# A decoder layer on one core: an inverse in two pieces, its gathers halved in number, tables made early, another order of loads

## The chip, the cores and the metric

The kernel is one launch on one core of a Trainium2 chip. The core's engines are TensorE (PE in the profile; PEld is its loading of weights), VectorE (DVE), ScalarE (ACT), GpSimd (POOL) and SyncE (SP), which issues the DMAs. The metric is the device time of the launch in microseconds (us), lower is better.

## The reference, cut to what matters

The kernel computes one decoder layer over 1,024 tokens of width 1,024 (depth 1, batch 1). A normed input is projected by one matrix of 3,136 columns. 448 of them feed multi-head latent attention with four heads, 1,664 feed an RWKV-7 recurrence of eight heads of 64 and the two low-rank inputs of its decay and rate, and 1,024 are a gate.

```python
u = rmsnorm(h, norm_pre_g[l])
p_mla, p_rw, z = jnp.split(u @ w_in[l], [MLA_COLS, MLA_COLS + RW_SHIFT_COLS], axis=-1)
c_q, c_kv, k_r = jnp.split(p_mla, [Q_LORA, Q_LORA + KV_LORA], axis=-1)
q  = rmsnorm(c_q, mla_q_norm_g[l]) @ mla_w_uq[l]      # split in nope and rope parts, per head
kv = rmsnorm(c_kv, mla_kv_norm_g[l]) @ mla_w_ukv[l]
y_mla = mla_attention(q_nope, apply_rope(q_rope, cos, sin), k_nope, apply_rope(k_r, cos, sin), v_mla)

ps = p_rw + (token_shift(p_rw) - p_rw) * rw_mu[l]
r, k, v, xw, xa = jnp.split(ps, ...)
w_log = -jax.nn.softplus(-(rw_w0[l] + jnp.tanh(xw) @ rw_w2[l])) - 0.5
decay, a = jnp.exp(-jnp.exp(w_log)), jax.nn.sigmoid(rw_a0[l] + xa @ rw_a2[l])
# kk: k * rw_k_k, normalised per head; k: k * (1 + (a - 1) * rw_k_a)
# per token and head: S = S * w + (S @ -kk) (kk * a)^T + v k^T ;  y = S @ r
y = wkv7_scan(r_h, heads(decay), k_h, v_h, kk, heads(a))
# y: group norm per head, plus (r * k * rw_r_k summed over the head) * v

y_cat = jnp.concatenate([y_mla, y_rw], axis=-1) * jax.nn.silu(z)
h = h + rmsnorm(y_cat @ w_out[l], norm_post_g[l])
```

## The kernel before, in words

The sequence is worked in two halves of 512 tokens. The recurrence isn't run token by token: it is cut into eight chunks of 64 tokens for each half, and within a chunk a 64x64 triangular system has to be inverted for each head. The recurrence, and with it the inverse, is done first for one half, then for the other; attention and the output come behind both.

**Order of the work.** `PROGRAM` (lines 132 to 136) is a string of operations in which they are written down; a scheduler (`schedule_with_timeline_sim`, line 42) then interleaves the instructions of all of them on every engine, by a simulation of its own. Once chosen, each engine's order is fixed, and an instruction that waits holds up whatever stands behind it on its engine. `BEHIND` (line 139) adds constraints: the operation named first is issued only after the last instruction that the other one returned. The letters, with the half as the first digit:

- `A` (`stage_a`, 165): loads four blocks of 128 tokens of x, norms them (eight scalings of 128x512 on VectorE, line 181), turns them with 32 transposes on TensorE (188), and writes the result as `uH` (ScalarE, 192, the rounded value) and `uL` (VectorE, 193, what the rounding lost), 16 pieces of each. Every projection multiplies in three terms: `uH` and `uL` by the weight's high part, `uH` by its low part.
- `X` (`lora_in`, 246): one projection (`proj`, 214: 24 matmuls of 512 columns, line 221, behind a load `wf`, a cast on ScalarE, 201, and eight subtractions on GpSimd, 211), its token shift (`v`, 228 to 231), a tanh (250) and the split `xw`, `xa` for the low-rank products (262, 263).
- `P` with the column block 0 to 3 (`prep`, 281): low-rank products, then the projections of k, r and v and their products on VectorE, which among others write `LS`. `E` (`units`, 358): masks and small matmuls by chunk (372) which make `LS`, `BK` and `AB`, the systems to be inverted; they are stored in `sa` in DRAM (395).
- `I` (`inverse`, 413): the elimination, 31 steps of two VectorE instructions (430, 432) over all 128 blocks of 32x32 at once, behind one load of `sa` with the blocks on the partitions (423). Then `sx` and `st`, the inverses and their transposes, are stored (434, 435) and gathered into `X1`, `X2T` and `AB` by twenty DMAs, ten for each of two groups of heads (442, 446, 449). Two rounds of 32x32 matmuls for each group (F, 459, and G, 466) and copies on VectorE and ScalarE (467, 468) make the off-diagonal blocks of `AB`.
- `C` (`chain`, 471): the eight chunks c0 to c7, one after the other, each in five groups of 64x64 matmuls (486, 493, 497, 503, 509); 497 is the first that reads the inverse. `N` (515): sums and powers of the group norm (the powers on GpSimd, 524). `G` (532): transposes and output of the recurrence.
- `M` (546), `T` (573): the attention's input projection, and its norm, turn and store to `cTd`. `Z` (584): a projection and silu of one gate block (588), stored to `zs`; `Y` (591) does two of them.
- `B` (664): the sine and cosine tables of the positions: 28 VectorE instructions (675 to 696) and two sines on ScalarE (697). `U` (702): loads `cTd` back, splits it (`cq` into `uH` and `uL`, 651), and scales the attention's weights. `K` (732): the turned key; `J` (`project`, 800, with matmuls at 814 and 821): the first head's queries and keys; `Q` (768): the turned queries; `S` (950): scores, probabilities (862 to 886), their product with the values (894) and the output product (942).

Tiles are named by tags of a pool, and a tag that is allocated again waits until its last users are done; `uH` and `uL` hold A0's result, then A1's, then U's. PSUM has the tags `pj` (four buffers), `wk` and `ch` (two each).

In the order before, TensorE meets A1's transposes between the inverse's matmuls, U's splits stand on ScalarE between the second inverse's copies, and the tables are made by VectorE behind the first half's elimination. SyncE issues everything in one queue, the twenty gathers in a row.

## Time and profile before

| what | value |
|---|---|
| runs shown | 776.36, 776.52, 782.18 us; median 776.52 |
| profiled execution | 775.78 us, span 772.4 us |
| mean granted TensorE clock | 0.933 |
| instructions | 13,874 |
| TensorE busy | 689.6 us, 89% of the span, 5,136 matmuls |
| VectorE busy | 454.0 us, 59%, 943 instructions |
| ScalarE busy | 345.8 us, 45%, 875 instructions |
| GpSimd busy | 331.1 us, 43%, 478 instructions |
| projections, high part of x (line 221, with `uH`) | 640 matmuls, 214.9 us |
| projections, low part of x (line 221, with `uL`) | 320 matmuls, 129.4 us |
| output product (line 942) on the chain that ended last | 11% of the span |

The span runs from the first to the last instruction that the profile records; the time of the execution holds 3.4 us more around it. A row of the timeline has the start, the busy time, the engine, the line, the operation, the tiles written and read with their shapes, and in brackets how long the engine stood idle ahead of it and on what. Of the matmuls' three terms, all are 128x128 by 512 columns and take 0.40 to 0.41 us each. Matmul ends are modelled, so that a TensorE that is busy at a low granted clock does less in its busy time; the clock is therefore read beside the busy time of each stretch.

### The profile page before, as it was taken

The page shows a single profiled execution, that of the slowest core. Times are in us where ns is not written, and L with a number is a line of the kernel's source. Part 1 is how long each engine was busy: PE and PEld are TensorE (multiplying, and loading weights), DVE is VectorE, ACT ScalarE, POOL GpSimd, SP SyncE. Part 2 cuts the span into 40 slices and gives each one's busy share as a digit, 9 for nine tenths or more (in the row PEclk, how much of TensorE's full clock was granted, in tenths as well). Part 3 has the DMA queues.
Part 4 walks back from the last instruction along what each step waited for, and adds up shares of the span by engine and source line. Part 5 has one row for each costly group of instructions (what it writes and reads, how often), then busy time and mean ns, then how long its engine had stood idle before and what let it go on. Part 6 is the DMA issues. An engine that isn't in the chain of part 4 may idle for free.

```text
span 772.4 us, 13874 instructions
## 1 busy us (share of the span) xinstructions
PE 689.6 (89%) x5136; PEld 564.9 (73%) x5136; DVE 454.0 (59%) x943; ACT 345.8 (45%) x875; POOL 331.1 (43%) x478
## 2 busy tenths in 40 slices
PE   2899998999858999859899989498899999899996
PEld 2677786787746777647778867386789988788885
DVE  4466675639829431684755593486777776644233
ACT  6646544428225452524634532332665475632221
POOL 6656555447712455453463652132512247432220
PEclk9899999999958899958999999598999999999998
DMA  6523332543570132252222554501231044253321
GB/s 185 150 80 89 91 81 65 145 122 100 167 158 19 28 109 58 55 116 60 54 68 72 138 157 124 164 15 30 57 75 49 22 126 121 72 169 121 123 81 55
DMA packets 118819, 72.84 MB, mean 94 GB/s; under 512 B 47072, under 2 KB 108256, under 8 KB 118752
## 3 DMA queue, kind: packets, MB, share of 16 engines
q1 hardware_dynamic: 118752, 71.96, 33.2%
q8 instruction: 40, 0.66, 0.3%
q14 instruction: 27, 0.22, 0.1%
HBM read 54.38 MB, written 17.56 MB: 93 GB/s over the span
## 4 chain that ended last, share of the span: by engine, by line
PE 36%; DVE 12%; DMA 4%; ACT 3%; POOL 2%; issue 2%; SPq 2%; DVEq 0%; ACTq 0%; POOLq 0%
PE pj L942 11%; PE pj L221 5%; PE pj L862 4%; PE ch L894 3%; DVE tmp L430 2%; PE pj L814 2%; DVE XA L432 2%; PE wk L883 2%; PE wk L372 1%; PE ch L503 1%; POOL w L211 1%; PE wk L509 1%; ACT wf L870 1%; PE pj L821 1%; DMA XA<-sa 1%
## 5 line engine op out<-in xcount | busy, mean ns | idle before, releaser
L221 PE MATMUL pj<-uH,w 128*128 128x512 f32 x640 | 214.9, 409 | 5.7 <-ACT sg L289 4.8
L211 POOL TENSOR_TENSOR w<-wf,w 128x256 fp32r<-128x256 f32 x168 | 140.0, 864 | 117.9 <-ACT w L201 106.8
L221 PEld LDWEIGHTS pj<-uH,w 128*128 128x128 f32 x640 | 121.8, 193 | 36.1 <-ACT sg L289 5.4
L221 PE MATMUL pj<-uL,w 128*128 128x512 f32 x320 | 129.4, 405 | 0.0
L221 PEld LDWEIGHTS pj<-uL,w 128*128 128x128 f32 x320 | 61.8, 193 | 14.2 <-issue 1.2
L201 ACT CAST w<-wf 128x1024 fp32r<-128x1024 f32 (+1 forms) x50 | 51.3, 1027 | 35.9 <-PE pj L556 17.3
L490 POOL TENSOR_TENSOR SD<-SV,Dg 64x128 f32<-64x128 f32 x64 | 30.0, 468 | 57.2 <-DVE SV L506 47.8
L874 POOL TENSOR_SCALAR wf<-wf,sm 128x128 f32<-128x128 f32 (+7 forms) x32 | 23.8, 747 | 62.2 <-DVE sm L873 45.4
L999 DVE TENSOR_TENSOR LS<-pj,LS 128x512 f32<-128x512 f32 x16 | 11.1, 691 | 45.1 <-ACT cq L998 44.4
L430 DVE TENSOR_TENSOR tmp<-XA 128x31 f32<-128x31 f32 (+15 forms) x62 | 28.1, 454 | 15.1 <-DMA XA<-sa 13.3
L885 ACT CAST BK<-wk 128x512 fp32r<-128x512 f32 (+3 forms) x48 | 22.6, 484 | 29.2 <-PE wk L883 27.4
L894 PE MATMUL ch<-BK,LS 128*128 128x256 f32 (+1 forms) x160 | 33.0, 288 | 0.2 <-ACT BK L885 0.2
L209 POOL TENSOR_TENSOR w<-wf,w 128x224 fp32r<-128x224 f32 x32 | 22.1, 722 | 25.5 <-ACT w L201 15.4
L886 DVE TENSOR_TENSOR AB<-wk,BK 128x512 fp32r<-128x512 f32 (+3 forms) x48 | 26.1, 551 | 8.5 <-ACT BK L885 8.1
L865 DVE TENSOR_REDUCE mx<-pj 128x1 f32<-128x512 f32 (+3 forms) x48 | 26.0, 552 | 8.5 <-PE pj L864 5.6
L870 ACT ACTIVATE wf<-pj,mx 128x512 f32<-128x512 f32 (+3 forms) x48 | 27.9, 588 | 5.2 <-DVE mx L867 5.0
L432 DVE TENSOR_TENSOR XA<-XA,tmp 128x31 f32<-128x31 f32 (+15 forms) x62 | 27.5, 443 | 1.9
L372 PEld LDWEIGHTS wk<-LS,pl 64*128 64x128 f32 x256 | 19.3, 187 | 12.2 <-issue 11.2
L998 ACT ACTIVATE cq<-pj 128x512 bf16<-128x512 f32 x16 | 9.6, 597 | 41.1 <-PE pj L942 41.1
L894 PEld LDWEIGHTS ch<-BK,LS 128*128 128x128 f32 x160 | 26.8, 197 | 0.9 <-ACT BK L885 0.5
L513 ACT COPY SV<-wk 128x128 f32<-128x128 f32 x32 | 6.9, 269 | 45.6 <-PE wk L509 45.6
L372 PE MATMUL wk<-LS,pl 64*128 64x128 f32 x256 | 24.8, 290 | 2.7 <-DVE LS L377 2.3
...
## 6 DMA issues: line engine op xcount, KB each, us to landing
...
```

Source lines behind the costliest of these rows:

```text
L201: S.copy(wh, wf)
L211: G.tensor_tensor(wl[:, sl], wf[:, sl], wh[:, sl].bitcast(F32), ALU.subtract)
L221: PE.matmul(ps, w_[:, kb], u_[:, kb], start=(n == 0), stop=(n == 23))
L372: PE.matmul(pE[e][:, ci], pl[ev[e], c4 + ci, 1 - e:3 - e].rearrange("p a b -> p (a b)"), LS[ev[e], c4 + ci, e, :], start=True, stop=True)
L430: V.tensor_tensor(t3, bc(At[:, j, j + 1:32].unsqueeze(2), (128, n, w)), bc(X[:, j, 0:w].unsqueeze(1), (128, n, w)), ALU.mult)
L432: V.tensor_tensor(X[:, j + 1:32, 0:w], X[:, j + 1:32, 0:w], t3, ALU.add)
L490: G.tensor_tensor(D_[ev[e]], SV[ev[e], c, e], bc(Dg[ev[e], :, c:c + 1], (64, 2, 64)), ALU.mult)
L862: PE.matmul(s_, l_, r_, start=(n == 0), stop=(n == 4 and b1 < e))
L870: S.activation(pr[:, b0:b1], sc[:, 0:b1 - b0], AF.Exp, bias=mx[:, 0:1], scale=-1.0, accum_out=sm[:, n5:n5 + 1])
L886: V.tensor_tensor(PL[:, b0:b0 + nb, o], pt[:, 0:nb], PH[:, b0:b0 + nb, o].bitcast(F32), ALU.subtract)
L894: PE.matmul(py[:, o], l_, r_, start=(j == 0 and n == 0), stop=(j == nk - 1 and n == 2), skip_group_check=True)
L942: PE.matmul(po[nb], l_, r_[:, ns], start=(k0 == 0 and k == 0 and n == 0), stop=(k0 == 4 and k == 3 and n == 2), skip_group_check=True)
```

## The change

1. **Order.** `PROGRAM` now has the tables (`B`) behind the first unit, `M0`, `Z03` to `Y06` and the second half's input `A1` behind the first inverse's `I0`, and only then `F0`, the end of the inverse, ahead of the chain `C0`; `T0` comes behind the chain's outputs; in the second half `Z10` and `Z12` stand one place earlier and `M1` is followed by `Z13`. `BEHIND` may name several, and an operation may return several instructions: `F0` is behind A1's last norm and last transpose, `Z11` behind the chain's last matmul, `U` behind the last copies of `F1`, `S` behind `U`'s last load; `B` is behind nothing any more.
2. **The inverse in two pieces**: `inverse` ends with the gathers, `finish` (`F`) holds the matmuls and copies.
3. **Ten gathers for twenty**: `AB` of both groups is one tile, `sa`, `sx` and `st` have the group inside, and each gather fetches both groups: two of 128 KB into `X1`, four of 64 KB into `X2T`, four of 128 KB into `AB`, the same bytes as before. The quadrants of `X2T` and `F` are counted `e * 2 + l` for `l * 2 + e`.
4. **A1's scalings** (eight) run on ScalarE, A0's stay on VectorE.
5. **Tiles**: the tables' scratch is `XA` for `q`; the transposes of the turned keys and queries take PSUM from `pj` for `wk`; the attention's low parts and the output's inputs are slices of one `AB` tile for two buffers.

What the scheduler makes of it, at three places. ScalarE in the opening, from the last piece of `uH` (line 192 before, 197 after) to the first gate's silu (`st`); `tab` is the table tile, `v` the shifted low-rank projection, `sq` the tanh. Before:

```order
L192 ACTIVATE uH_98<-pj_219,vec_65 128x256
L228 ACTIVATE v_272<-pj_247,omm_76 128x512
L201 CAST w_350<-wf_348 128x1024
L230 ACTIVATE v_272<-plast_86,v_272,vec_65 128x1
L231 COPY plast_86<-pj_247 128x1
L250 ACTIVATE sq_277<-v_272 64x512
L588 ACT_TABLE_LOAD
L588 ACTIVATE st_318<-pj_293 128x512
```

After:

```order
L197 ACTIVATE uH_98<-pj_219,vec_65 128x256
L707 ACT_TABLE_LOAD
L707 ACTIVATE tab_589<-tab_589 128x256 x2
L234 ACTIVATE v_272<-pj_247,omm_76 128x512
L207 CAST w_349<-wf_347 128x1024
L236 ACTIVATE v_272<-plast_86,v_272,vec_65 128x1
L237 COPY plast_86<-pj_247 128x1
L256 ACT_TABLE_LOAD
L256 ACTIVATE sq_277<-v_272 64x512
L599 ACT_TABLE_LOAD
L599 ACTIVATE st_318<-pj_293 128x512
```

The two sines and their table stand ahead of `v`, and the tanh has a table load of its own.

TensorE around the second half's input: Y06's last matmuls (602 before, 613 after), A1's transposes (188, 193), the matmuls F and G of the first inverse (459 and 466, 470 and 477) and T0's transposes (579, 590). Before:

```order
L602 MATMUL pj_2563<-uH_98,w_2556 128x256
L579 MATMUL pj_2668<-cst_64,cq_2390 128x128 x3
...
L579 MATMUL pj_2695<-cst_64,cq_2426 128x128 x3
L459 MATMUL ch_1530<-XA_1509,AB_323 32x32
L188 MATMUL pj_2730<-cst_64,v_2702 128x128
...
L188 MATMUL pj_2730<-cst_64,sg_2716 128x128
L459 MATMUL ch_1530<-XA_1509,AB_323 32x32 x31
L188 MATMUL pj_2739<-cst_64,v_2702 128x128
...
L466 MATMUL ch_1564<-XA_1509 32x32 x16
L466 MATMUL ch_1583<-XA_1509 32x32 x16
L459 MATMUL ch_1602<-XA_1509,AB_327 32x32 x32
```

After:

```order
L613 MATMUL pj_1863<-uH_98,w_1856 128x256
L193 MATMUL pj_1994<-cst_64,v_1966 128x128
...
L193 MATMUL pj_2085<-cst_64,r_2045 128x128
L470 MATMUL ch_2094<-XA_1547,AB_321 32x32 x32
L590 MATMUL pj_2824<-cst_64,cq_1690 128x128 x3
...
L477 MATMUL ch_2128<-XA_1547 32x32 x16
L477 MATMUL ch_2147<-XA_1547 32x32 x16
L590 MATMUL pj_2851<-cst_64,cq_1726 128x128 x3
L227 MATMUL pj_2866<-uH_98,w_2860 128x512
```

All of A1's transposes stand ahead of the first matmul that reads a gather, T0's have moved from ahead of the inverse's matmuls to between them, and the projection of `X1` (227) begins behind the first group's G, with the second group's F and G within it. On SyncE the twenty gathers stood in one row behind `sx`, `st` and one gate's store; now they are ten, in one row behind `sx`, a weight load, `st`, a gate's store and one more weight load `wf`. Further down, the first half's chunks c3 to c7 have no projection between them in TensorE's new order, and `Z11`, the low-rank product and the projections of `P11`, and `Z12` stand behind c7; before, projections stood among c2 to c4, and c5 to c7 were nearly bare.

ScalarE around the end of the second inverse: its copies into `AB` (468, 478), U's splits (651, 661), the turned key's copies (760 after), and the first copy of the chain, `Rs`. Before:

```order
L651 CAST uH_5284<-cq_5310 128x256
L651 CAST uH_5284<-cq_5314 128x256
L651 CAST uH_5284<-cq_5318 128x256
L468 COPY AB_2921<-ch_4230 32x8x32
L651 CAST uH_5284<-cq_5322 128x256
L651 CAST uL_5285<-cq_5326 128x256
L468 COPY AB_2921<-ch_4249 32x8x32
L651 CAST uL_5285<-cq_5330 128x256
L488 COPY Rs_4275<-ch_4273 128x128
```

After:

```order
L478 COPY AB_2904<-ch_4172 32x8x32
L478 COPY AB_2904<-ch_4191 32x8x32
L478 COPY AB_2904<-ch_4244 32x8x32
L760 CAST XA_5358<-pj_5361 64x512
...
L760 CAST XA_5358<-pj_5382 64x512
L478 COPY AB_2904<-ch_4263 32x8x32
L661 CAST uH_5262<-cq_5264 128x256
L661 CAST uH_5262<-cq_5268 128x256
L498 COPY Rs_4289<-ch_4287 128x128
```

U's splits have gone behind the last of the copies; what stands between these is the turned key.

The diff, cut to its core:

```diff
@@ -124,19 +124,22 @@
             name = op.rstrip("0123456789")
-            with tc.issue_after(done[BEHIND[op]].ins) if op in BEHIND else contextlib.nullcontext():
+            with contextlib.ExitStack() as stack:
+                for first in BEHIND.get(op, "").split():
+                    for ins in done[first]:
+                        stack.enter_context(tc.issue_after(ins.ins))
                 done[op] = ops[name](*(int(i) for i in op[len(name):]))
...
 PROGRAM = (
-    "A0 X0 Z00 P00 E00 Z01 P01 E01 Z02 P02 E02 P03 E03 I0 C0 N00 G00 N01 G01 M0 Z03 Z04 Z05 Y06 T0 A1 B X1",
-    "P10 E10 Z10 P11 E11 Z11 P12 E12 P13 E13 I1 C1 N10 G10 N11 G11 M1 Z12 T1 Z13 Z14 Z15 Z16 Z17 U K J Q0",
+    "A0 X0 Z00 P00 E00 B Z01 P01 E01 Z02 P02 E02 P03 E03 I0 M0 Z03 Z04 Z05 Y06 A1 F0 C0 N00 G00 N01 G01 T0 X1",
+    "P10 Z10 E10 Z11 P11 E11 Z12 P12 E12 P13 E13 I1 F1 C1 N10 G10 N11 G11 M1 Z13 T1 Z14 Z15 Z16 Z17 U K J Q0",
     "Q1 Q2 Q3 S",
 )
...
-BEHIND = {"X0": "A0", "B": "I0"}
+BEHIND = {"X0": "A0", "F0": "A1", "Z11": "C0", "U": "F1", "S": "U"}
@@ -176,22 +177,27 @@
-                last[0] = E["rstd"](ss[:, 0:1], 1.0 / D)
+                norm = E["rstd"](ss[:, 0:1], 1.0 / D)
                 for i in range(2):
-                    V.tensor_scalar(xh[i], xh[i], ss[:, 0:1], 1.0, ALU.mult, ALU.mult)
+
+                    if h:
+                        S.activation(xh[i], xh[i], AF.Copy, scale=ss[:, 0:1])
+                    else:
+                        V.tensor_scalar(xh[i], xh[i], ss[:, 0:1], 1.0, ALU.mult, ALU.mult)
...
                     for q in range(2):
-                        PE.transpose(ps[:, kk, q * 128:(q + 1) * 128], xs[q][kb // 4][:, (kb % 4) * 128:(kb % 4 + 1) * 128], ident)
+                        turned = PE.transpose(ps[:, kk, q * 128:(q + 1) * 128], xs[q][kb // 4][:, (kb % 4) * 128:(kb % 4 + 1) * 128], ident)
...
+        return norm, turned
@@ -266,14 +272,15 @@
+        AB = alloc(P1, (128, 2, 2, NCH, 128), "AB")
...
-            AB=alloc(P1, (128, 2, NCH, 128), "AB", bufs=2),
+            AB=AB[:, :, g],
...
-        ) for _ in range(2)]
+        ) for g in range(2)]
         return dict(
-            g=gs,
+            g=gs, AB=AB,
@@ -416,7 +423,7 @@
-        rows = "g e b l c i j -> (g e b l c) i j"
+        rows = "e b l g c i j -> (e b l g c) i j"
@@ -433,40 +440,43 @@
         SP.dma_start(sx.rearrange(rows), X)
         SP.dma_start(st.rearrange(rows), At)
-        FX = alloc(P1, (128, 2, 4, NCH, 32), "XA")
+
+        FX = alloc(P1, (128, 2048), "XA")
+        X1 = FX[:, 0:1024].rearrange("p (l g c j) -> p l g c j", l=2, g=2, j=32)
+        X2T, F = (FX[:, o:o + 512].rearrange("p (g c j) -> p g c j", g=2, j=32) for o in (1024, 1536))
+        for e in range(2):
+            SP.dma_start(X1[e * 64:e * 64 + 32].rearrange("p l g c j -> p (l g c) j"),
+                         sx[e, 0].rearrange("l g c i j -> i (l g c) j"))
+        for e, l in ((0, 0), (1, 0), (0, 1), (1, 1)):
+            q = (e * 2 + l) * 32
+            SP.dma_start(X2T[q:q + 32].rearrange("p g c j -> p (g c) j"), st[e, 1, l].rearrange("g c i j -> i (g c) j"))
+        for b in range(2):
+            for e in range(2):
+                p0 = e * 64 + b * 32
+                SP.dma_start(gt["AB"][p0:p0 + 32, :, :, :, b * 32:b * 32 + 32].rearrange("p l g c j -> p (l g c) j"),
+                             st[e, b].rearrange("l g c i j -> i (l g c) j"))
+        gt["XF"] = X1, X2T, F
+
+    def finish(h, gt):
+
+        X1, X2T, F = gt["XF"]
         for g in range(2):
             AB = gt["g"][g]["AB"]
-            X1, X2T = FX[:, g, 0:2], FX[:, g, 2]
-            for e in range(2):
-                p0 = e * 64
-                SP.dma_start(X1[p0:p0 + 32].rearrange("p l c j -> p (l c) j"),
-                             sx[g, e, 0].rearrange("l c i j -> i (l c) j"))
-                for l in range(2):
-                    q = l * 2 + e
-                    SP.dma_start(X2T[q * 32:q * 32 + 32], st[g, e, 1, l].rearrange("c i j -> i c j"))
-                for b in range(2):
-                    p0 = e * 64 + b * 32
-                    SP.dma_start(AB[p0:p0 + 32, :, :, b * 32:b * 32 + 32].rearrange("p l c j -> p (l c) j"),
-                                 st[g, e, b].rearrange("l c i j -> i (l c) j"))
...
-                    q = l * 2 + e
+                    q = (e * 2 + l) * 32
...
-                    PE.matmul(pF[q * 32:q * 32 + 32, c], AB[r, l, c, 32:64], X1[r, l, c], start=True, stop=True)
-            V.tensor_copy(F, pF)
+                    PE.matmul(pF[q:q + 32, c], AB[r, l, c, 32:64], X1[r, l, g, c], start=True, stop=True)
+            V.tensor_copy(F[:, g], pF)
...
-                end = V.tensor_copy(AB[0:32, l, :, 32:64], pG[0:32])
-                S.copy(AB[64:96, l, :, 32:64], pG[64:96])
-        return end
+                        q = slice((e * 2 + l) * 32, (e * 2 + l) * 32 + 32)
+                        PE.matmul(pG[e * 64:e * 64 + 32, c], F[q, g, c], X2T[q, g, c], start=True, stop=True)
+                ends = (V.tensor_copy(AB[0:32, l, :, 32:64], pG[0:32]), S.copy(AB[64:96, l, :, 32:64], pG[64:96]))
+        return ends
@@ -506,11 +516,12 @@
-                    PE.matmul(pY[ev[e], g, l], AB[ev[e], l, c, 64:128], SV[ev[e], c, e, l], start=False,
-                              stop=True, skip_group_check=True)
+                    end = PE.matmul(pY[ev[e], g, l], AB[ev[e], l, c, 64:128], SV[ev[e], c, e, l], start=False,
+                                    stop=True, skip_group_check=True)
...
+        return (end,)
@@ -674,7 +684,7 @@
-        ak = alloc(P2, (128, 2, 8, 32), "q")
+        ak = alloc(P2, (128, 2, 8, 32), "XA")
@@ -726,8 +736,9 @@
-            SP.dma_start(wf, w_ukv[:, sl])
+            end = SP.dma_start(wf, w_ukv[:, sl])
             scaled(ukH[:, sl], ukL[:, sl], wf, V_KVG)
+        return (end,)
@@ -743,7 +754,7 @@
-                ps = wk((64, 512))
+                ps = pj((64, 512))
@@ -922,7 +935,7 @@
-        w_ = alloc(P2, (128, 2, 4, 128), "AB", F32R, bufs=2)
+        w_ = lows[0][:, t % 2, 0:4].rearrange("p a (b c) -> p (a b c)", c=128).rearrange("p (a b c) -> p a b c", a=2, c=128)
@@ -950,6 +963,7 @@
+        lows.append(alloc(P2, (128, 2, 8, 256), "AB", F32R))
@@ -964,7 +978,7 @@
-                                      alloc(P2, (128, 8, 256), "AB", F32R, bufs=2))
+                                      lows[0][:, i // 2 % 2])
```

16 lines of the change are left out of this document (5 added, 11 removed).

## The prediction

> **What bounds the kernel now.** The run behind the profile took 775.8 us: a span of 772.4 and 3.4 around it; the median shown is 776.5, or 0.7 more. I read first the windows by stage. The columns are the stretch and its length, busy time (and instructions) of PE, PEld, DVE, ACT and POOL, then the granted TensorE clock, DMA share and GB/s.
>
> ```profile
> 0.00:40.00 40.00, 23.64 (x97) 19.23 (x98) 17.80 (x41) 25.07 (x50) 26.07 (x49) 0.91 0.62 172
> 208.00:236.00 28.00, 17.37 (x326) 14.02 (x326) 10.98 (x31) 10.29 (x24) 6.66 (x10) 0.57 0.63 161
> 236.00:262.00 26.00, 23.17 (x205) 17.17 (x204) 17.17 (x42) 11.15 (x29) 9.49 (x14) 0.87 0.08 22
> 262.00:300.00 38.00, 38.00 (x326) 28.96 (x325) 14.71 (x29) 15.04 (x34) 19.29 (x29) 1.00 0.24 70
> 300.00:322.00 22.00, 20.27 (x283) 16.13 (x283) 9.15 (x25) 10.60 (x37) 9.62 (x21) 1.00 0.20 50
> 322.00:357.00 35.00, 23.63 (x156) 19.37 (x157) 25.83 (x43) 13.19 (x30) 17.10 (x20) 0.66 0.37 87
> 430.00:476.00 46.00, 42.59 (x222) 34.75 (x221) 33.41 (x74) 20.82 (x51) 25.13 (x36) 0.96 0.50 148
> 476.00:498.00 22.00, 11.68 (x308) 9.14 (x306) 7.18 (x19) 7.20 (x21) 0.58 (x1) 0.71 0.59 145
> 498.00:562.00 64.00, 57.60 (x758) 46.57 (x759) 47.95 (x118) 26.90 (x93) 23.07 (x39) 0.89 0.19 48
> ```
>
> TensorE is the bound nearly everywhere, so I count what it loses: length minus busy time times clock. That is 18.1, 5.8, 0, 1.7 and 19.4 us in the five stages from 208 to 357, together 45.0; and 5.1, 13.7 and 12.7, together 31.5, from 430 to 562. These two stretches hold the two inverses and the chains behind them. Next I read the waits of PE (total, times, longest):
>
> ```profile
> PE ch L486 <- ACT AB L468: 8.7, 3, 7.8
> PE ch L459 <- DMA XA<-sx: 8.6, 3, 5.2
> PE pj L262 <- DVE xw L254: 2.4, 1, 2.4
> ```
>
> The chain (L486) waits for a copy of the inverse's result on ScalarE, the inverse for its gathers, and in the opening the low-rank product for `xw`.
>
> **The opening: tables made early.** The angle tables' 28 VectorE operations, now between 231 and 246, move into the first 30 us, between the `uL` pieces, and ScalarE makes the two sines before the first projection's result `v`. Here are ScalarE and TensorE in the opening, and three table rows at their old place:
>
> ```profile
> 28.59 0.69 ACT L228 ACTIVATE v<-pj,omm 128x512 f32<-128x512 f32 x1 [5.22 <-PE pj L221]
> 31.23 1.28 ACT L588 ACT_TABLE_LOAD   x1
> 32.53 0.60 ACT L588 ACTIVATE st<-pj 128x512 f32<-128x512 f32 x1
> 34.61 0.76 PE L262 MATMUL pj<-xw,lora 128*128 128x512 f32 x1 [2.39 <-DVE xw L254]
> 23.04 0.88 DVE L193 SCALAR_TENSOR_TENSOR uL<-pj,vec,uH 128x256 fp32r<-128x256 f32 x2 [0.89 <-ACT uH L192]
> 231.88 1.27 DVE L681 TENSOR_SCALAR q<-cst,posf 128x32 f32<-128x32 f32 x8
> 235.75 0.42 DVE L687 SCALAR_TENSOR_TENSOR q<-q 128x256 f32<-128x256 f32 x1
> 245.74 0.29 DVE L696 TENSOR_SCALAR tab<-tab 128x256 f32<-128x256 f32 x1
> ```
>
> Eight small ones take 1.3 and nineteen larger ones 0.3 to 0.4 each: an estimate of 8 us of VectorE, of which about 4 fall behind the last `uL` piece (23.92). So the second sine ends near 30.5, `v` starts 2 late, and one more table load (1.28) stands ahead of the tanh. VectorE recovers 1 of it, as the tanh was ready before VectorE came to it. The product at 34.61, and all behind it, comes about 3 us later; bounds 1 (the tables fit into VectorE's idle time) and 6 (every table operation doubled beside GpSimd). **+3.**
>
> The Trainium skill ("ScalarE: Activation LUTs", What ACT_TABLE_LOAD costs) gives a load 1283 ns and a drain of 1380 ns more. The trace agrees on the load, but the next activation starts 1.30 after it, so no drain is seen; with it the term would be 4.4 and the forecast 754.
>
> **The second half's input ahead of the inverse's end (208 to 357).** Now TensorE's transposes of A1 stand behind F-matmuls that wait for gathers; the change puts all 32 ahead of them, and SyncE issues ten gathers for twenty. Rows of SyncE, the list of DMAs (KB each, us to landing), VectorE, GpSimd, ScalarE and TensorE:
>
> ```profile
> 210.15 0.33 SPq L435 DMA_DIRECT2D st<-XA  x1
> 212.84 0.32 SPq L442 DMA_DIRECT2D XA<-sx  x1
> XA<-sx SPq DMA_DIRECT2D x8, 64.0 KB, 2.2
> 187.60 0.48 DVE L181 TENSOR_SCALAR sq<-sq,ss 128x512 f32<-128x512 f32 x1
> 207.10 6.34 POOL L211 TENSOR_TENSOR w<-wf,w 128x256 fp32r<-128x256 f32 x8 [4.78 <-ACT w L201]
> 18.65 2.98 ACT L192 ACTIVATE uH<-pj,vec 128x256 fp32r<-128x256 f32 x7 [1.15 <-PE pj L188]
> 254.31 0.63 PE L221 MATMUL pj<-uH,w 128*128 128x512 f32 x1
> ```
>
> A1 then runs at the pace of its 16 pieces, 0.43 each on ScalarE (2.98 for 7): from 208 to about 216. VectorE's elimination, rid of eight scalings of 0.48 (now ScalarE's), ends some 4 earlier, so `st` is issued near 206 instead of 210.15 and has landed, 2.7 later as now, near 208.8. The gathers now stand on SyncE behind a weight load whose buffer comes free at the middle of that GpSimd row, near 210.3: they start near 210.7 and the first lands 2.2 later, still under A1's pieces. So the load ahead costs nothing; it would cost 2 if A1 were shorter. The copies of T0, the F-matmuls and X1 follow, and the key projection of P10, at 254.31 now, starts 18 us earlier, though with one and a half chain chunks fewer behind it.
>
> That moves what covers what. In the new order c3 to c7 have no projection between them, while Z11, the low-rank product, three projections of P11, and Z12 come behind c7, where TensorE now loses 19.4. The rows:
>
> ```profile
> 304.79 0.68 PE L497 MATMUL ch<-Rs,AB 64*64 64x64 f32 x16 [0.26 <-ACT Rs L488]
> 308.68 0.72 PE L497 MATMUL ch<-Rs,AB 64*64 64x64 f32 x16
> 320.69 0.62 PE ch L503 x16
> 312.21 1.67 DVE L322 SCALAR_TENSOR_TENSOR LS<-k,vec,sg 64x512 f32<-64x512 f32 x2 [0.41 <-PE wk L493]
> 313.91 1.39 DVE L329 TENSOR_TENSOR LS<-r,sg 64x512 f32<-64x512 f32 x2
> 331.66 4.52 POOL L524 TENSOR_TENSOR gss<-gss,mhalf 128x16 f32<-128x16 f32 x1
> 363.96 5.92 PE pj L221 x25
> ```
>
> A bare chunk lasts 3.9 (304.79 to 308.68) for five groups of 0.62, so each loses 0.8. A projection of 24 matmuls is 5.7 of cover. TensorE's losses from 208 to P12 I then put at: A1 4.5 (TensorE idle for about half of its 8); inverse, T0 and first chunk at low clock 5; the wait for `xw` behind X1 and slow matmuls after it 5 (6.0 from `v` to the product in the opening, less 2.5 of chain work); five bare chunks 4; `LS` written within c7 3 (1.67 and 1.39); behind c7 4.5, as Z11 covers 5.7 of the two powers and reduces on GpSimd and the rest is queued projections. Sum 26 for 45. Bounds: 18 and, if nothing is won, 45; I take 26. **-19.** Z12 (5.7) is only work moved; taken out of the second inverse's cover it costs nothing there if that stage is set by latency, as the next part says, and 5.7 if not.
>
> **The second inverse (430 to 562).** Now ScalarE holds the inverse's last copies behind splits that wait for loads queued behind twenty gathers:
>
> ```profile
> 472.78 0.32 SPq L442 DMA_DIRECT2D XA<-sx  x1
> 484.14 0.91 SPq L589 DMA_DIRECT2D zs<-st  x2
> 490.83 0.80 ACT L651 CAST uL<-cq 128x256 fp32r<-128x256 f32 x2 [6.88 <-DMA cq<-cTd]
> 494.32 0.36 ACT L468 COPY AB<-ch 32x256 f32<-32x256 f32 x1
> 496.80 1.12 PE L497 MATMUL ch<-Rs,AB 64*64 64x64 f32 x16
> 497.85 1.22 PE L814 MATMUL pj<-uH,pl 128*128 128x512 f32 x2
> ```
>
> The change puts U behind F1. Twenty gathers are issued from 472.78 until ahead of 484.14, a good half microsecond each; ten take about 5. With 2.2 to land, two rounds of F-matmuls and copies end near 481.5 and L497 comes near 482.5 instead of 496.80. J (L814) needs U's eight loads and `w_uq`, and comes only 4 earlier; c0 and c1 run before it. Z13 to Z17 end near 473, when the gathers begin, so the missing Z is not missed. Losses: 5 up to 476 as before; 6 around the F-matmuls; 4.5 in c0 and c1; 9 to 562, for 12.7 (no key transposes between the last chunks). Together 24.5 for 31.5; bounds 18 and 31.5. **-7.**
>
> The attention and output behind 562 keep their order; one tile in two slots for two tiles changes no wait that I find: 0. Sum: 775.8 + 3 - 19 - 7 = **753** (bounds of the terms: 741 to 780).
>
> **Rivals.** *The gap behind the chain stays*: the powers (4.52) and VectorE's serial 20 us of masks, norms and `LS` writes hold E10 and E11, and the projections queued in TensorE stand behind them. VectorE is at 25.83 of 35 there, which speaks for it; that the queue has 24 matmuls between any two waits speaks against. Then 15 of the 19.4 stay: 768. *The gathers take as long in ten*: the same bytes, in DMAs twice as large; DMA share in 476 to 498 is 0.59, not full, so partly. The second inverse then gains 1 for 7: 759. *More is won*: the lower ends, 18 and 18, give 738. *No difference*, the order on each engine different but the same waits elsewhere: 776. *Slower, by the clock*: from A1 to c7 TensorE has some 62 us of full-clock work in short pieces (X1 and four projections of 5.7, eight chunks of 3.1, 9 of transposes and small products). At the 0.57 granted in 208 to 236 it would take 47 more, less 5 counted: 795; it decides against the change where the clock there is below 0.69. For it: that row, at three fifths busy, and 0.66 in 322 to 357. Against: 1.00 in 300 to 322 with bare chunks.
>
> The Trainium skill ("TensorE: Matmul & The Clock Gate", Part 1) has the clock halve after an idle window of some 3.4 us and return after as much busy time. The trace agrees as far as 322 to 357 was slow around its long waits; by the rule c0 to c7 stay at full clock, and the slower rival falls.
>
> **How the numbers follow.** Forecast 0.60 (742 to 765), the gap stays 0.13, gathers no faster 0.13, more won 0.06, no difference 0.04, slower 0.04. The likeliest is 753. The range 734 to 769 leaves out little but the last two and part of the gap's. Within 1% (768.8 to 784.3) a measurement here tells little from no change; faster by more: 0.60, 0.13, 0.06 and 0.08 of the gap's 0.13 make 0.87; same 0.05 and 0.04, so 0.09; slower by more 0.04, the clock's case.
>
> **What would show it.** In the changed profile: the first low-rank matmul near 37.5 instead of 34.61; A1's transposes in one run, X1's first matmul near 223 (236.02 now); P10's key projection near 239; c3 to c7 about 4 us apart; P12's low-rank product near 347 (357.26 now) with Z12 done; no wait of the chain for ScalarE's copy of `AB`; the second c0 near 473; the first scores some 23 earlier. I am wrong if the elimination on VectorE ends after Y06's last matmul, since all of A1's `uL` pieces stand behind it; if the weight load ahead of the gathers is issued after 214; or if TensorE's loss behind c7 is above 10.

## The result, and the profile after

The changed kernel takes 752.87 us (median of 4 runs, 751.78 to 756.70) against 776.75 of the kernel before beside it (4 runs, 776.36 to 782.18): a ratio of 0.9686, with a 95% interval of 0.9629 to 0.9742. The forecast was 753. The profiled execution took 753.94, a span of 752.2 and 1.7 around it (3.4 in the profiled execution before; the other executions of all runs have 1.7 to 3.0).

First the windows of the changed kernel, in the columns of the prediction's first fence, cut at its own landmarks:

```profile
0.00:40.00 40.00, 20.10 (x80) 15.77 (x81) 27.57 (x67) 24.04 (x49) 21.03 (x43) 1.00 0.49 141
212.50:224.00 11.50, 8.43 (x173) 7.50 (x171) 7.69 (x19) 8.40 (x19) 2.94 (x6) 0.85 1.10 236
224.00:236.66 12.66, 9.07 (x171) 6.98 (x168) 4.11 (x8) 5.64 (x13) 3.24 (x4) 0.91 0.53 139
236.66:240.40 3.74, 3.01 (x23) 2.43 (x22) 2.27 (x4) 1.40 (x4) 1.36 (x3) 0.50 0.31 70
240.40:276.88 36.48, 36.48 (x324) 27.70 (x322) 15.09 (x28) 16.26 (x37) 17.42 (x25) 0.94 0.23 66
276.88:300.00 23.12, 19.74 (x382) 16.40 (x380) 13.46 (x38) 9.43 (x38) 10.73 (x26) 0.98 0.10 26
300.00:321.00 21.00, 21.00 (x129) 16.41 (x129) 13.08 (x20) 7.18 (x15) 13.90 (x15) 0.94 0.58 140
321.00:342.03 21.03, 20.54 (x124) 16.04 (x123) 14.79 (x24) 12.68 (x28) 13.59 (x19) 1.00 0.36 94
416.00:457.00 41.00, 37.38 (x196) 30.64 (x195) 33.84 (x74) 19.28 (x49) 22.64 (x32) 0.92 0.42 130
457.00:474.00 17.00, 13.55 (x320) 11.05 (x320) 6.45 (x15) 6.08 (x16) 0.00 (x0) 0.78 0.52 108
474.00:543.00 69.00, 62.79 (x780) 51.19 (x777) 49.31 (x126) 31.71 (x116) 26.51 (x43) 0.86 0.28 76
```

Length minus busy time times clock is 4.3 for A1, 6.6 for the inverse and the wait for `xw`, 2.2 up to c3, 3.8 in the bare chunks, 1.8 behind c7: 18.7 where the kernel before lost 45.0. Of the 45.0, 26.6 were idle time of TensorE and 18.5 the clock; now it is 11.3 and 7.4. The granted clock is 0.94 to 1.00 from 240 to 342; before it was 0.66 in the last 35 us of that stage. Around the second inverse the three rows give 6.6, 6.4 and 15.0.

Then PE's waits in the changed kernel (total, times, longest). The two long ones for the inverse's gathers and for ScalarE's copy of `AB` are gone, though 4.0 us of short waits for that copy are left; those for `uL` and `xw` have grown, both in the opening. Of the 8.1 for `uL`, 5.4 are A0's pieces (3.0 before) and 2.7 are A1's.

```profile
PE pj L193 <- DVE uL L198: 8.1, 3, 2.8
PE pj L268 <- DVE xw L260: 4.6, 2, 3.9
PE ch L496 <- ACT AB L478: 4.0, 4, 1.7
```

The opening of the changed kernel on VectorE, ScalarE and TensorE: table instructions between the `uL` pieces, then the second sine, which ends the wait of `v`, and one more table load ahead of the tanh.

```profile
17.66 3.59 DVE L691 TENSOR_SCALAR XA<-cst,posf 128x32 f32<-128x32 f32 x5
27.96 0.47 DVE L198 SCALAR_TENSOR_TENSOR uL<-pj,vec,uH 128x256 fp32r<-128x256 f32 x1
33.71 0.42 ACT L707 ACTIVATE tab<-tab 128x256 f32<-128x256 f32 x1 [2.19 <-DVE tab L706]
34.03 0.67 ACT L234 ACTIVATE v<-pj,omm 128x512 f32<-128x512 f32 x1
36.13 1.28 ACT L256 ACT_TABLE_LOAD   x1
...
40.00 0.77 PE L268 MATMUL pj<-xw,lora 128*128 128x512 f32 x1 [3.87 <-DVE xw L260]
```

Its two inverses on SyncE and TensorE: the store of `st`, a weight load, the first gathers, the first F-matmuls (L470), X1 (L227), P10's low-rank product (L268); then the second half's gathers and the first L507, which reads its inverse.

```profile
211.28 0.32 SPq L442 DMA_DIRECT2D st<-XA  x1
212.57 0.68 SPq L204 DMA_DIRECT2D wf<-in_w_in_dram  x1
216.46 0.93 SPq L448 DMA_DIRECT2D XA<-sx  x2
...
220.85 0.74 PE L470 MATMUL ch<-XA,AB 32*32 32x32 f32 x62 [0.38 <-DMA XA<-sx]
224.00 0.48 PE L227 MATMUL pj<-uH,w 128*128 128x512 f32 x1
238.52 0.80 PE L268 MATMUL pj<-xw,lora 128*128 128x512 f32 x1 [0.73 <-DVE xw L260]
...
458.09 0.93 SPq L448 DMA_DIRECT2D XA<-sx  x2
461.42 4.03 SPq L456 DMA_DIRECT2D AB<-st  x4
472.86 1.47 PE L507 MATMUL ch<-Rs,AB 64*64 64x64 f32 x16 [0.33 <-ACT Rs L498]
```

What the first of these gathers waited for on SyncE (total, times, longest):

```profile
SPq L448 <- DMA st<-XA: 3.2, 1, 3.2
```

It waited for `st` to land, 5.1 us behind its issue at 211.28, and not for the weight load, which was issued at 212.57. Before, `st` landed 2.6 behind its issue, and so it does in the second half of the changed kernel; in the first half another weight load stands 1.1 ahead of it (210.15), and the DMA engines are busy for 0.99 of the time until it lands. Whether that load is the cause was not tried.

The stages of every profiled execution, in us, by the same landmarks. The columns are: the start of the first low-rank product; from there to the load of `sa` of the first half; the elimination (load of `sa` to store of `sx`); from Y06's last matmul to P10's low-rank product; from there to P12's; from the second half's load of `sa` to the fourth head's projection; from there to the first output product; the span.

| kernel | first product | to `sa` | elimination | to P10 | P10 to P12 | `sa` to head 4 | to output | span |
|---|---|---|---|---|---|---|---|---|
| before | 34.6 | 132.9 | 41.1 | 44.5 | 104.8 | 190.0 | 54.9 | 772.4 |
| changed | 40.0 | 132.6 | 37.0 | 26.2 | 103.5 | 180.1 | 58.0 | 752.2 |
| changed, again | 39.7 | 133.1 | 36.9 | 27.4 | 104.1 | 178.9 | 54.6 | 750.8 |
| tables behind X0 | 36.8 | 134.9 | 37.0 | 25.4 | 103.9 | 182.1 | 55.2 | 748.5 |
| twenty gathers | 39.2 | 135.6 | 37.8 | 28.8 | 104.2 | 182.8 | 55.8 | 758.0 |
| U unbound | 40.2 | 132.8 | 36.9 | 27.3 | 103.1 | 179.4 | 55.1 | 749.9 |
| A1 in its old place | 40.5 | 135.9 | 36.7 | 37.4 | 101.2 | 180.2 | 54.2 | 762.0 |
| Z11 unbound | 40.0 | 133.0 | 36.9 | 26.8 | 115.9 | 183.1 | 55.7 | 766.3 |
| scalings on VectorE | 40.2 | 135.6 | 42.9 | 30.7 | 102.3 | 181.6 | 53.0 | 753.9 |
| before, ten gathers | 34.3 | 135.9 | 41.0 | 40.9 | 117.2 | 185.5 | 57.5 | 781.3 |
| before, gates kept back | 33.9 | 135.7 | 42.0 | 47.1 | 95.8 | 187.3 | 56.0 | 768.5 |
| tables behind E01 | 34.3 | 139.0 | 36.6 | 28.3 | 104.2 | 180.1 | 54.9 | 751.9 |
| tables behind E00 | 34.7 | 139.8 | 37.0 | 26.2 | 102.5 | 181.1 | 55.2 | 748.8 |
| tables in the chain | 33.7 | 132.8 | 36.4 | 25.8 | 102.2 | 180.6 | 54.7 | 740.9 |

Z12 (5.7) lies in the column P10 to P12 of all rows but two: before, and before with ten gathers, have it behind the second `sa`.

### The profile page after: what moved, and what is told of

It is laid out like the page before. It is cut to its first block, busy times and chain, and to the rows that moved or that the text cites. A ratio compares the mean times of both kernels' runs of the same rounds, so it can differ in the third digit from the quotient of the medians.

```text
span 752.2 us, 13837 instructions
## 1 busy us (share of the span) xinstructions
PE 686.9 (91%) x5136; PEld 564.2 (75%) x5136; DVE 460.8 (61%) x935; ACT 353.4 (47%) x885; POOL 335.7 (45%) x478
## 3 DMA queue, kind: packets, MB, share of 16 engines
q1 hardware_dynamic: 118432, 71.96, 34.3%
## 4 chain that ended last, share of the span: by engine, by line
PE 39%; DVE 11%; ACT 4%; DMA 3%; issue 2%; POOL 2%; SPq 0%; DVEq 0%; ACTq 0%; POOLq 0%
PE pj L955 12%; PE pj L227 7%; PE pj L873 4%; PE ch L905 3%; PE pj L825 2%; PE wk L894 2%; PE wk L379 1%; PE ch L513 1%; PE pj L832 1%; DMA lora<-in_w_out_dram 1%; PE pj L789 1%; PE wk L519 1%; DVE LS L329 1%; DVE XA L439 1%; DVE BK L396 1%
## 5 line engine op out<-in xcount | busy, mean ns | idle before, releaser
L227 PE MATMUL pj<-uH,w 128*128 128x512 f32 x640 | 218.2, 413 | 3.0 <-ACT sg L296 2.3
L217 POOL TENSOR_TENSOR w<-wf,w 128x256 fp32r<-128x256 f32 x168 | 145.1, 893 | 102.4 <-ACT w L207 92.9
L227 PEld LDWEIGHTS pj<-uH,w 128*128 128x128 f32 x640 | 123.6, 195 | 33.3 <-ACT sg L296 2.5
L227 PE MATMUL pj<-uL,w 128*128 128x512 f32 x320 | 130.0, 406 | 0.0
L227 PEld LDWEIGHTS pj<-uL,w 128*128 128x128 f32 x320 | 62.7, 196 | 13.8 <-issue 0.7
L207 ACT CAST w<-wf 128x1024 fp32r<-128x1024 f32 (+1 forms) x50 | 51.3, 1025 | 29.0 <-PE pj L567 20.3
L437 DVE TENSOR_TENSOR tmp<-XA 128x31 f32<-128x31 f32 (+15 forms) x62 | 27.7, 447 | 15.6 <-DMA XA<-sa 13.8
L876 DVE TENSOR_REDUCE mx<-pj 128x1 f32<-128x512 f32 (+3 forms) x48 | 25.8, 551 | 7.6 <-PE pj L875 4.1
L383 DVE TENSOR_TENSOR AB<-wk,cs 64x512 f32<-64x512 f32 x16 | 10.9, 684 | 28.6 <-PE wk L379 28.6
```

Of the source, the lines that this page charges most:

```text
L207: S.copy(wh, wf)
L217: G.tensor_tensor(wl[:, sl], wf[:, sl], wh[:, sl].bitcast(F32), ALU.subtract)
L227: PE.matmul(ps, w_[:, kb], u_[:, kb], start=(n == 0), stop=(n == 23))
L437: V.tensor_tensor(t3, bc(At[:, j, j + 1:32].unsqueeze(2), (128, n, w)), bc(X[:, j, 0:w].unsqueeze(1), (128, n, w)), ALU.mult)
```

## The experiments

Runs that were timed together share a chip and the runs of the kernel before; ratios are to those. The changed kernel has 0.9686 (0.9629 to 0.9742) and, on the chip of the last four, 0.9643 (0.9608 to 0.9678), so a difference under some 0.5% between runs that were not timed together says nothing, and the stages of the table are what is read.

**Tables behind X0.**

```diff
-BEHIND = {"X0": "A0", "F0": "A1", ...
+BEHIND = {"X0": "A0", "B": "X0", "F0": "A1", ...
```

> The changed kernel with one constraint more: the tables (B) are issued only behind the splits of the first low-rank input (the last of xa), so their 28 VectorE instructions and two sines leave the first 30 us and meet the projections of P00 and P01. In the changed kernel the first low-rank product starts at 40.00, 5.4 later than before, and the next ones (68.11, 100.21, 124.50) are all 5.1 later too. Theory 'the tables hold the opening, and nothing gives it back': the first low-rank product is at 34.6 to 35.6, the fourth near 119.5, and the run near 747.5 (5.4 less than 752.9). Rival 'VectorE pays elsewhere': 8 us of VectorE and four table loads land in front of P00's chain; the first product is at 35 but the second and fourth are no earlier than 66.5 and 123, and the run is 751 to 753.

750.52 us, ratio 0.9651 (0.9600 to 0.9701). The first product came at 36.79 and the fourth at 123.43 (124.50 in the changed kernel, 119.40 before). The rival holds, with the run a little below its 751 to 753: five of the eight small table instructions stood between the two splits of `xw`, the others in P00's chain; 3.2 were won and 2.1 paid back at once.

**Twenty gathers again.** The two tiles `AB`, the layout and the gathers' loops are those of the kernel before, with the split in two pieces kept.

```diff
-            SP.dma_start(X1[e * 64:e * 64 + 32].rearrange("p l g c j -> p (l g c) j"),
-                         sx[e, 0].rearrange("l g c i j -> i (l g c) j"))
...
+                SP.dma_start(X1[p0:p0 + 32].rearrange("p l c j -> p (l c) j"),
+                             sx[g, e, 0].rearrange("l c i j -> i (l c) j"))
...
```

> The changed kernel with twenty gathers again: two tiles AB, the DRAM layout, the quadrants and the loops of the gathers as before, group by group; the split in two pieces and the order stay (TensorE's order differs only in a few rows near the second half's c0 and at the very end). Theory 'it is the number of DMAs': a row of twenty is issued in about 11 us instead of 5; the second group's F-matmuls of the second inverse come 3 to 5 later than now (465.70), its c0 near 476 to 478 instead of 472.86, the first inverse loses 1 to 3 more, and the run is 757 to 760. Rival 'it is the bytes': the gathers end when they do now, and the run is 752 to 754. Third, 'the chain's cover hides it': the gathers end later but J and the key's transposes fill the gap; c0 later by 4, the run by less than 2.

760.38 us, ratio 0.9752 (0.9716 to 0.9787). The gathers of the second inverse on SyncE, first and last, in this kernel:

```profile
463.92 0.32 SPq L449 DMA_DIRECT2D XA<-sx  x1
...
474.30 0.98 SPq L456 DMA_DIRECT2D AB<-st  x2
```

A row of twenty takes 11.4 (463.92 to 475.28), the ten of the changed kernel 7.4 (458.09 to 465.45), so to issue a gather with twice the bytes costs 0.74 on the average for 0.57. From the store of `sx` to the second c0 it is 22.1 (459.96 to 482.03) for 19.1 and, in the repeat, 17.8; to the fourth head 2.7 to 3.9 more, and 1.4 to 2.6 more at P10; against either execution the two make 5.3. So some 5 of the 7.5 are the gathers'. The stretch ahead of `sa` has 2.5 to 3 more, where no gather has been issued yet; the clock is at half for 10.2 us there, for 3.4 in the changed kernel. The first theory holds, and the third is refuted, as the run to the fourth head is not level; the 760.38, just above the first theory's 757 to 760, has the stretch ahead of `sa` in it.

**U and S unbound.**

```diff
-BEHIND = {"X0": "A0", "F0": "A1", "Z11": "C0", "U": "F1", "S": "U"}
+BEHIND = {"X0": "A0", "F0": "A1", "Z11": "C0"}
```

> The changed kernel without the constraints of U behind F1 and S behind U: on ScalarE all of U's splits (cq into uH, uL) stand between and ahead of the second inverse's copies into AB again, while the ten gathers stay. Theory 'the splits hold the copies': the chain's first matmuls wait for ScalarE's copy of AB by 5 or more, the second half's first L507 comes near 479 instead of 472.86, and the run is 757 to 760. Rival 'ten gathers alone did it': with half the DMAs ahead of them the loads of cq land in time, the splits are through before the copies are due, c0 comes within 1.5 of now, and the run is 752 to 754, or lower since J has its inputs earlier.

754.25 us, ratio 0.9688 (0.9635 to 0.9740). ScalarE and TensorE around the second c0 of this kernel:

```profile
470.51 0.40 ACT L661 CAST uL<-cq 128x256 fp32r<-128x256 f32 x1 [3.16 <-DMA cq<-cTd]
...
476.84 0.36 ACT L478 COPY AB<-ch 32x256 f32<-32x256 f32 x1
...
478.67 1.19 PE L825 MATMUL pj<-uH,pl 128*128 128x512 f32 x2 [0.72 <-DVE XA L761]
481.74 0.69 PE L507 MATMUL ch<-Rs,AB 64*64 64x64 f32 x8
```

Splits that wait for their loads again hold ScalarE's copies of `AB`, and c0 comes at 481.74, 8.9 later (8.0 to 9.3 behind the store of `sx`): the mechanism that the prediction named. But J (L825) starts 5.0 earlier (478.67 for 483.68), since its inputs are split, and from `sa` to the fourth head nothing is lost (179.4 for 180.1 and 178.9). So the constraint is worth nothing by itself: what it takes from the chain's wait it gives to J's.

**A1 in its old place.**

```diff
-    ... I0 M0 Z03 Z04 Z05 Y06 A1 F0 C0 N00 G00 N01 G01 T0 X1",
+    ... I0 F0 C0 N00 G00 N01 G01 M0 Z03 Z04 Z05 Y06 T0 A1 X1",
-BEHIND = {"X0": "A0", "F0": "A1", ...
+BEHIND = {"X0": "A0", ...
```

> The changed kernel with the first half's program in the old order (I0 F0 C0 N G M0 Z03 Z04 Z05 Y06 T0 A1 X1) and no constraint of F0 behind A1: A1's transposes stand among the inverse's matmuls on TensorE as before; tables, gathers, Z11 and Z12, U and ScalarE's scalings stay changed. Theory 'A1 behind the gathers is what cost': P10's low-rank product comes some 12 to 18 later than 238.52 (250 to 256), P12's some 15 later than 342.03, and the run is 766 to 772. Rival 'the filled gap behind c7 is what gained': the place of A1 is worth 5 or less in the end, since the chain then has more projections between its chunks; P12's within 6 of 342.03 and the run 755 to 759.

764.47 us, ratio 0.9809 (0.9763 to 0.9855), between the two theories. The windows from Y06's end to P10's low-rank product, here and in the changed kernel:

```profile
215.00:252.36 37.36, 29.16 (x456) 22.72 (x454) 15.37 (x35) 15.98 (x40) 10.88 (x17) 0.73 0.44 109
```

```profile
212.37:238.52 26.15, 18.76 (x357) 15.55 (x355) 13.59 (x28) 14.83 (x35) 7.67 (x12) 0.85 0.74 172
```

A1 in pieces behind the gathers costs 11.2 there; 2.3 come back by P12, since part of the second chunk already lies in that stretch.

**Z11 unbound.**

```diff
-BEHIND = {"X0": "A0", "F0": "A1", "Z11": "C0", "U": "F1", "S": "U"}
+BEHIND = {"X0": "A0", "F0": "A1", "U": "F1", "S": "U"}
```

> The changed kernel without the constraint of Z11 behind the first half's chain: TensorE's order then has Z11, the low-rank product and parts of P11 and Z12 between the chunks c3 to c7 again, as in the kernel before, and fewer of them behind c7; the rest is as in the changed kernel. So far A1's old place cost 11.6 of the 23.7 between the medians, twenty gathers 7.5, U's old place nothing, and the tables took some 2 to 5, so about 7 are not accounted for. Theory 'the projections kept back fill the gap behind c7': TensorE idles behind c7 again, P12's low-rank product comes 4 to 8 later than 342.03, and the run is 757 to 761. Rival 'only moved': what the bare chunks c3 to c7 lose (3.8 by the windows) is won back, P12's comes within 2 of 342.03 and the run is 751 to 754.

767.13 us, ratio 0.9842 (0.9813 to 0.9870): more than the theory asked. The last window of the stage, and PE's longest wait between P10 and P12:

```profile
316.00:355.33 39.33, 29.13 (x203) 23.55 (x201) 27.08 (x46) 16.20 (x41) 15.21 (x22) 0.70 0.33 78
```

```profile
PE pj L406 <- DVE q L338: 3.5, 1, 3.5
```

The gap behind c7 is back: 39.33 less 29.13 times 0.70 is 18.9 lost, where the changed kernel loses 1.8 in the 42 us behind 300. TensorE idles for only 10.2 of it, in pieces of 3.5 and less; the other 8.7 are the clock of 0.70.

**Scalings on VectorE.**

```diff
-                    if h:
+                    if False:
                         S.activation(xh[i], xh[i], AF.Copy, scale=ss[:, 0:1])
```

> The changed kernel with A1's eight scalings of 128x512 on VectorE again. They are 0.48 each, so VectorE has 3.8 more to do between the load of sa (172.64) and the store of sx (209.66). Theory 'the elimination is late then and the gathers with it': sx is stored 3 to 4 later behind the load of sa, the first F-matmuls come 2 to 3 later than 220.16, and the run is 2 to 4 longer (755 to 757). Rival 'hidden behind A1': the gathers now wait for a weight load until 216.46 and A1's transposes last until 219.81, so the first F-matmul moves by less than 1 and the run is 752 to 754.

759.77 us, ratio 0.9748 (0.9721 to 0.9774). The elimination takes 42.9 for 37.0, and A1 itself, whose `uL` pieces stand behind it on VectorE, now holds TensorE (PE's longest wait from 213 to 246):

```profile
PE pj L193 <- DVE uL L198: 5.2, 1, 5.2
```

P10 comes 3.3 to 4.5 later behind Y06's end. It is the first theory in its direction, with the wait at A1 rather than at the gathers and a run above its 755 to 757; 3.0 to 3.2 of that lie ahead of `sa`, where the clock is at half for 10.2 us and in the changed kernel for 3.4.

**Before, with ten gathers alone** (one tile `AB`, the layout, the quadrants, the slices of `lows`).

> The kernel before with the ten gathers alone (one tile AB for both groups, the layout with the group inside, the quadrants, the attention's slices of AB); its program, constraints, tables and scalings stay as they were, though the scheduler moves single rows. In the changed kernel the twenty gathers cost 7.5 of the medians. Theory 'each DMA of the row delays what stands behind it, in any order': the gain is there without the new order too, 4 to 8 (769 to 773). Rival 'the gathers are on the path only where A1 doesn't cover them': before, the first inverse has A1's transposes among its matmuls and the second has U's splits ahead of its copies, which wait for loads behind the gathers; then the first gains nothing, the second 1 to 3, and the run is 774 to 777.

781.18 us, ratio 1.0035 (1.0012 to 1.0058). Both theories missed. The gathers gain: P10 comes 3.6 earlier behind Y06's end, and `sa` to the fourth head takes 185.5 for 190.0. But the scheduler also moved single rows in the chain: the last products of c7 come at 327.50 for 313.55, behind a projection that stood behind them before. In the last 38.6 us ahead of P12 TensorE then loses 23.6, where it loses 19.7 in the last 38.3 of the kernel before:

```profile
330.00:368.60 38.60, 24.95 (x169) 20.89 (x170) 26.80 (x45) 13.66 (x32) 15.39 (x20) 0.60 0.34 79
```

P10 to P12 takes 117.2 for 104.8. What this run says of the gathers is in their two stages; its total is that of another order in the chain.

**Tables behind E01.**

```diff
-    "A0 X0 Z00 P00 E00 B Z01 P01 E01 Z02 ...
+    "A0 X0 Z00 P00 E00 Z01 P01 E01 B Z02 ...
-BEHIND = {"X0": "A0", "F0": "A1", ...
+BEHIND = {"X0": "A0", "B": "E01", "F0": "A1", ...
```

> The changed kernel with the tables issued behind the second unit E01 (and written there in the program): 28 VectorE instructions and two sines between some 85 and 120, where the windows of the changed kernel show TensorE without a gap and VectorE busy for 39 of 56. Behind the splits of X0 they still cost 4.0 of 5.1 at the fourth low-rank product, 2.3 of it since eight small ones stood between xa and xw and 1.8 within P00. Theory 'VectorE has room there': first low-rank product at 34.6 to 35.0, the fourth at 119.4 to 120.0, and the run 747 to 749 (4 to 6 less than 752.9). Rival 'no free place for them': VectorE's work of the units is later by 2 to 4 there, the load of sa comes no earlier than 171, and the run is 750 to 753.

756.12 us, ratio 0.9696 (0.9674 to 0.9718). The rival holds, with a run above its 750 to 753: the fourth product is at 119.12, 5.4 earlier, but the tables ran from 118.87 to 136 and the load of `sa` comes at 173.27, later than in the changed kernel. So the place between 85 and 120, which the theory meant, was not tested here. PE's longest wait from 119 to 214, which is 1.7 long in the changed kernel:

```profile
PE pj L406 <- DVE q L338: 4.9, 1, 4.9
```

**Tables in the chain, tables behind E00, the changed kernel again** (timed together). For the first, `B` is written behind P11 and named behind C0; for the second it is named behind E00.

> The changed kernel with the tables issued among the first half's first chunks: written behind P11 and named behind C0, they are placed by the scheduler from the first chunk's products on (the scratch tile is free behind the inverse's last matmuls), some 240 to 256, where the changed kernel has TensorE without a gap (36.48 of 36.48 from 240.40 to 276.88) and VectorE busy for 15.09. So far they cost 5.4 in the opening, 4.0 behind X0 and 5.4 within E03 (54.15 for 48.14 from the fourth low-rank product to the load of sa). Theory 'VectorE is on the path only where TensorE has no queue': first low-rank product near 34.6, P10's at 233 to 234, P12's at 336 to 338, span 745 to 748 (750.0 to 754.9 in the changed kernel's executions). Rival 'the chain pays': the chain's VectorE instructions (its state, its copies) wait behind the tables', c1 and c2 come 3 to 5 later behind P10's product and the span stays 750 to 753.

> The changed kernel with the tables issued behind the first unit E00's last copy on VectorE, some 91 to 100. TensorE has no gap from 68 to 124 and VectorE idles for 17 of 56 there, 3.5 of it in one piece ahead of the token shift of P01's v. Theory as in the experiment before: first low-rank product near 34.6, fourth at 119.1 to 119.9, the load of sa 48.2 behind that, the span 745 to 748. Rival 'VectorE is serial through the units': its 8 us push E01 and P02, and as behind E01 the 5 us come back as a wait of TensorE for VectorE before sa is loaded (50 to 54 for 48.2); the span stays 750 to 753.

> The changed kernel once more, unchanged, to time the two before it against and to see how far one execution differs from the next. In the profiled execution of the changed kernel the attention's end (from the fourth head's projection to the first output product) took 57.97 at a clock of 0.91, against 54.2 to 55.8 in the four experiments with the same code there. Theory 'that was this execution's clock': it takes 55 to 56 here and the span is near 750. Rival 'it is the change's': 58 again and a span near 752. The median is expected at 751 to 755.

746.90 us for the tables in the chain, ratio 0.9583 (0.9551 to 0.9616), against 752.08 for the changed kernel again, 0.9643 (0.9608 to 0.9678), and 753.18 behind E00, 0.9649 (0.9617 to 0.9682). The first is the best kernel of this study; the two intervals touch, but its landmarks are 4.7 to 7.1 earlier than the repeat's from the fourth product to P10. C0 returns the chain's last matmul, behind 290, yet the tables run from 226.97 to 243.26, around the first chunk (c0 at 229.07): the constraint did not hold back instructions of another engine. The windows of this kernel:

```profile
0.00:33.74 33.74, 18.63 (x80) 15.08 (x81) 16.44 (x40) 21.45 (x45) 20.83 (x44) 1.00 0.61 174
118.26:166.53 48.27, 44.24 (x261) 35.66 (x260) 26.45 (x40) 19.73 (x47) 22.04 (x34) 1.00 0.36 102
232.69:270.39 37.70, 37.70 (x324) 28.87 (x324) 21.93 (x48) 18.89 (x40) 19.28 (x27) 0.93 0.20 58
```

TensorE has no gap from 232.69 to 270.39, with VectorE busy for 21.93 where the changed kernel has 15.57 in the same stretch (238.52 to 276.88); nothing is paid back. Behind E00, where the tables run from 86.20 to 103.37, the 5 us of the opening come back, by the rival: 27.3 for 24.3 from the third low-rank product to the fourth, 2.4 of it waits of TensorE for VectorE, and 52.1 for 48.1 to 49.9 from there to `sa`, 0.9 of it more idle time and 3.3 a clock of 0.93. And the repeat has 54.6 from the fourth head to the output: the 58.0 of the profiled execution was that execution's.

**Before, with the gates kept back alone.**

```diff
-    "P10 E10 Z10 P11 E11 Z11 P12 E12 P13 ... M1 Z12 T1 Z13 ...
+    "P10 Z10 E10 Z11 P11 E11 Z12 P12 E12 P13 ... M1 Z13 T1 ...
-BEHIND = {"X0": "A0", "B": "I0"}
+BEHIND = {"X0": "A0", "B": "I0", "Z11": "C0"}
```

> The kernel before with one part alone: in the second half Z10, Z11 and Z12 stand one place earlier (Z12 with P12) and Z11 is issued behind the first half's chain; A1 stays among the inverse's matmuls, gathers, tables, scalings and U as before. Taking this constraint out of the changed kernel cost 14.2 of the medians, putting A1 back 11.6, the gathers back 7.5, the scalings 3 to 7: more than the 23.7 to 25 there are. Theory 'each is worth its price by itself': P12's low-rank product, 5.7 of Z12 taken off, comes 10 to 14 earlier than 357.26 (so 349 to 353 with it), and the run is 764 to 769. Rival 'they only work together': without A1 in its new place the chain starts as late as before, the projections kept back leave the chunks bare and the gap is only moved: P12's later than 355, and the run is 773 to 778.

767.78 us, ratio 0.9844 (0.9802 to 0.9887): 12.5 of the medians, by the first theory. The end of the stage has no gap left:

```profile
308.00:352.64 44.64, 43.57 (x277) 34.08 (x275) 31.65 (x47) 21.46 (x50) 28.38 (x35) 0.93 0.40 98
```

P10 to P12 takes 95.8 for 104.8, with Z12 in it, while P10 itself comes 2.6 later behind Y06's end. Order alone, in one stretch, is half of what the whole change gains.

## Why the prediction was right, point by point

The number was right to 0.2 us, and the mechanisms of its terms held in the main. That it came so close is luck: the three terms were off by 2 to 7, stages that the sum had at nothing moved by up to 3, and all this balanced. From the profiled executions, stage by stage: opening +5.4; to Y06's end -1.0; from there to P12 -19.7; to the second `sa` +1.7; to the fourth head -9.9; to the output +3.1; the rest +0.2; outside the span -1.6. That is 775.8 to 753.9.

**Opening, +3.** Measured +5.4, inside the bounds 1 to 6. The second sine ahead of `v` was right: `v` starts at 34.03 for 28.59, all of the 5.4. The table load ahead of the tanh cost nothing: from `v` to the product it is 5.97 for 6.02. Mis-sized was how far the tables push A0's own pieces. The last `uL` piece ends at 28.43 for 23.92 (TensorE's waits for `uL` in the first 25 us are 5.4 for 3.0), and 5.2 of tables follow for the 4 that I had put, so the sine ends at 34.13 and not near 30.5. The 28 instructions keep VectorE busy for 12.4 us here and for 8.1 in their old place, from which I had taken my 8; five of the small ones take 3.59 where all eight took 1.27. The part is a loss: the tables in the chain take it back, 5.2 between the two medians.

**A1 ahead of the inverse's end and the gap behind c7, -19.** Measured -25.4 (19.7 and Z12's 5.7), past the expected value and close to the lower bound of 18 for what is left to lose. A1 was right (4.3 for 4.5), X1 came at 224.00 for 223, P10's key projection at 240.40 for 239, c3 to c7 3.9 to 5.3 apart. The inverse, the wait for `xw` and the slow matmuls after it lost 8.8 for 10 (6.6, and 2.2 up to c3), the chunks 3.8 for 7, the gap 1.8 for 4.5. So the two terms that were mis-sized are the last ones, and both were waits: in c7 I had put 3 for `LS`, and PE's only long wait there is 1.07; behind c7 I had put 4.5, and TensorE idles for 0.5 of the 42 us behind 300. The slow clock around the inverse was sized nearly right: c0 and the low-rank product run at 0.50. Each cause was taken out by itself: A1's place is worth 11.2 up to P10 and 8.9 up to P12, the order behind c7 12.4 (Z11 unbound) or 14.7 with Z12 (before with the gates kept back). Up to P12 the single prices (A1's place 8.9, the order 13.0, the gathers and the scalings 3.4 each) make 28.7 of the 25.4 that the stage won; reckoned against the repeat they make 21.1 of 23.5. So they add up to the whole as nearly as two executions agree.

**The elimination and SyncE's order.** It was 4.1 shorter, as said, by the scalings. I had it end near 205 since I left the opening's delay out; `st` was issued at 211.28 for 206. The weight load ahead of the gathers was issued at 212.57, short of the 214 that I named as a mark of failure. Yet the gathers began at 216.46, not 210.7: beside the opening's delay, `st` took 5.1 to land and not the 2.7 that I had carried over. The expectation of the scalings' experiment is wrong to put this wait down to a weight load. A1's last transposes began at 219.81, and PE waited 0.38 for the second gather, so the cover was just enough, with nothing to spare.

**The second inverse, -7.** c0 was at 472.86 for 473, yet the losses there fell by only 4.9, inside the bounds: 28.0 by the three rows above, which reach to the second head, for 32.9 before (31.5 to 562 and 1.4 more up to the second head). Two of the reasons were given one price, and only one earns it: the gathers do (2.7 to 4.5), though ten take 7.4 and not 5; U behind F1 moves c0 by 8.9 and wins nothing, as J has less cover then. I counted c0 as the end of the wait, where J, which needs all of U, is as much what TensorE's queue stands behind.

**Attention, 0.** 58.0 for 54.9 in the profiled execution, 54.6 in the repeat: 0 holds.

**Rivals.** The gap that stays is what Z11 unbound shows, without the constraint; the gathers that are no faster are refuted by twenty; the slower clock by the windows. By the Trainium skill ("TensorE: Matmul & The Clock Gate", Part 1) the bare chunks were to keep full clock, and the row 276.88 to 300 has 0.98: the trace agrees. It does not agree for c0, which the prediction put under the same rule: the row 236.66 to 240.40 has 0.50, behind waits of 1.6. Nor were the waits in the kernel before, from 322 to 357, as long as that rule asks: 3.2 and less, at a clock of 0.66. The fifth part of the change, the tiles, was never taken out by itself; what it is worth is not shown.
